# A decoder trunk with its residual stream turned round: tokens instead of features on partitions, and norms applied before the products

## The chip, the cores and the metric

One core of a Trainium2 chip runs the whole program. The metric is device time in microseconds of one execution, the median over runs of the same program. The core has a matrix engine (TensorE, PE in the profile; PEld is its loading of stationary operands), VectorE (DVE), ScalarE (ACT), GpSimd (POOL) and SyncE (SP), whose queue issues most transfers.

## The reference

512 tokens of 1024 features run through two layers in float32. Each layer is a half-step SwiGLU FFN (width 2816), a mixer, and another half-step FFN; every sub-layer has an RMS norm before it and one behind it, and is added to the residual stream. The mixer of layer 0 is a gMLP (chunked causal gating over 128 tokens, 16 groups); the mixer of layer 1 is multi-head latent attention (8 heads) whose keys and values come from the stream after layer 0.

```python
def rms_norm(x, g):
    y = x32 * lax.rsqrt(jnp.mean(x32 * x32, axis=-1, keepdims=True) + RMS_EPS) * g
...
for layer in range(DEPTH):
    f = swiglu(rms_norm(h, ffn_pre_g[layer, 0]), w_gate, w_up, w_down)
    h = h + 0.5 * rms_norm(f, ffn_post_g[layer, 0])
    n = rms_norm(h, mix_pre_g[layer])
    m = gmlp_mixer(n, ...) if layer < N_A_LAYERS else mla_mixer(n, k_nope, k_rope, v, ...)
    h = h + rms_norm(m, mix_post_g[layer])
    f = swiglu(rms_norm(h, ffn_pre_g[layer, 1]), w_gate, w_up, w_down)
    h = h + 0.5 * rms_norm(f, ffn_post_g[layer, 1])
    if layer == N_A_LAYERS - 1:
        k_nope, k_rope, v = shared_kv(h, ...)
```

## The kernel before

**Layout.** Everything lives with features on partitions: the residual stream `hall` is 8 chunks of 128 features by 512 tokens. A weight chunk of 128 x 128 is TensorE's stationary operand and 512 (or 256) tokens move.

**Precision.** Each float32 operand is split exactly into a high and a low float32r part; `mm3` makes a product of three TensorE instructions (high by high, high by low, low by high). A *unit* of weights is a transfer of some 512 KB into a raw buffer (`wr`, WR = 3 of them), then one ScalarE cast (`wh`) and one VectorE subtraction (`wl`) into split buffers (WS = 6 pairs). Activations share a pool of 59 slots of 128 x 512 (`a` in the profile).

**Order.** The program is a list of `Item`s, run in order by `Flow.drive`. Each names the units that it loads. `Flow` keeps an estimate of when each engine finishes each instruction. Ahead of each product, `Flow.reach` advances whatever waiting generator is due by that estimate, and `Flow.feed` splits units up to AHEAD = 4 items ahead where a split buffer is free and VectorE and ScalarE have little to do. `flow.hold` stops such splitting while a root is awaited. On the chip each engine then runs its instructions in the order that comes out, waiting on semaphores.

**Pre-norms are late.** `gained` splits h times the gain, not normed; the products of the next sub-layer start on that. The norm's scalar per token (`Norm`: R along tokens on all partitions, r by token, e) is made meanwhile: `Squares` sums squares of chunks (ScalarE, then adds on GpSimd), `token_mean` sums over features with TensorE (`mean` in the profile), `rsqrt` runs five small steps on GpSimd (`y`, `nt`, `r`), and `spread` lays the scalars along tokens with TensorE (`ident,r`). `glu`, `v_out`, `u_out` and the latent multiply by R or r behind the products. SwiGLU's up branch is not multiplied: the output then is f r, and the post-norm takes e = eps / r^2 in place of its epsilon.

**Seams.** `Boundary` is what lies between two sub-layers; there are b0 (input) to b6 (output), and five seams b1 to b5 have work on both sides. `project` computes a sub-layer's output, in groups of hidden features (FGROUPS) for an FFN. In the last group, HELD chunks of output (4, or 3 behind a mixer) keep their weights and run in two halves of 256 tokens, A and then B. `Boundary.finish` is started behind each half: token_mean, root, spread (`half,y`; `ident,y`), then for each chunk the post-norm, the residual sum, `gained` and the square for the next norm. While it runs for A, TensorE does the held chunks of B; while it runs for B, TensorE does the first three pairs of columns of the next FFN on A (`p` and `q` in `ffn`; `q` is loaded early into activation slots), or the first columns of the next mixer. At the end, `store` writes the last half by chunks of features.

**Shared keys.** `Shared.run` splits the stream after layer 0 again with `kv_norm`'s gain and multiplies by R behind the product.

Of the kernel before, what the change touches and what calls it, by code (L numbers as in the profile page):

```python
# [33 lines left out]
FGROUPS = ((0, 8), (8, 15), (15, 22))  # L34
# [23 lines left out]
for _name, _w in (  # L58
    ("ffn_pre", 32), ("ffn_post", 32), ("mix_pre", 16), ("mix_post", 16), ("kv_norm", 8),
    ("kv_a", 2), ("q_norm", 4), ("ln_g", 16), ("ln_b", 16), ("inv_freq", 1),  # L60
):
    COLS[_name] = _n
    _n += _w
# [13 lines left out]
def cost(engine, name, aps):  # L77
    """About how long an instruction takes, in microseconds."""
    n = max(int(np.prod(x.shape[1:])) for x in aps)
    if engine == "PE":  # L80
        n = int(np.prod(aps[0].shape[1:]))
        return max(n * (1 if aps[1].dtype in (F32R, BF16) else 4) / 2370.0, 0.03)
# [28 lines left out]
class Flow:  # L111
    """The order of the program. Work that waits for other engines is a generator, which yields what it
    waits for: a condition (a callable), tensors (a list) or an engine that has less than so much to
    do (a pair). What engines do is followed by an estimate of each instruction's time."""
# [28 lines left out]
    def place(self, key, t, us):  # L143
        """Takes the first time from t on in which the engine has nothing to do."""
# [14 lines left out]
    def idle(self, key, lead):  # L159
        """When the engine has less than lead to do."""  # L160
# [34 lines left out]
    def reach(self, t):  # L195
        """TensorE's next instruction can start at t: do what is due before."""
# [13 lines left out]
    def drive(self, items, fetch, parts):  # L210
        """Run the items. Units are fetched, and split into parts, before their time where there is room."""
# [48 lines left out]
class Parts:  # L260
    """The two parts of each chunk of a tensor, and which halves of the tokens have been written."""
# [13 lines left out]
def decoder_kernel(ctx: ExitStack, tc: tile.TileContext, a: dict, out: bass.AP):  # L275
# [14 lines left out]
    # names given, units split  # L290
# [29 lines left out]
    # tables and clocks of the engines that the first products wait for  # L320
# [19 lines left out]
    half = const.tile([P, P], F32, name="half")  # L340
    GP.tensor_scalar(half, ident, 0.5, None, op0=ALU.mult)
# [10 lines left out]
    hall = const.tile([P, NK, S], F32, name="h")  # L352
    h = [hall[:, c, :] for c in range(NK)]

    def load_x(lo, hi_, chunks=range(0, NK, 2)):
        xT = a["xT"].rearrange("(c p) t -> p c t", p=P)
        for c in chunks:
            nc.sync.dma_start(hall[:, c : c + 2, lo:hi_], xT[:, c : c + 2, lo:hi_])
            flow.dma += 0.75
            flow.write(hall[:, c : c + 2, lo:hi_], flow.dma + 2.0)  # L360

# [7 lines left out]
    def parts(raw, src, shape, spare=False):  # L369
        """The parts of each of a unit's chunks; `spare` units take room of activations."""  # L370
# [20 lines left out]
    def mm3(ps, w, x, start, stop):  # L391
        """ps += w^T x from the parts of w (stationary) and x (moving)."""
# [30 lines left out]
    def rsqrt(x, n, out=None):  # L423
        """1 / sqrt of a few columns."""
# [14 lines left out]
    def token_mean(acc, lo, hi_, n):  # L439
        """Means of acc's columns over n features, by token on partitions."""  # L440
# [5 lines left out]
    def spread(c, n, diag):  # L446
        """Per-token scalars (token on partition, one column a tile) along the free axis, on all partitions."""
# [8 lines left out]
    class Squares:  # L456
        """Sums of chunks' squares."""
# [14 lines left out]
    class Norm:  # L472
        """Scalars of a pre-norm: R along tokens on all partitions, r by token, e = eps / r^2."""

        def __init__(self):
            self.R = slot()
            self.r = small(NT, "r", 3)
            self.e = small(NT, "e", 3)
            self.squares = Squares()
            self.have, self.wide = set(), set()  # L480

        def finish(self, lo, hi_):
            n = (hi_ - lo) // P
            j0 = lo // P
# [6 lines left out]
            y = rsqrt(x, n, self.r[:, j0 : j0 + n])  # L491
            V.tensor_scalar(self.e[:, j0 : j0 + n], x, RMS_EPS, None, op0=ALU.mult)
            self.have.add(lo)
# [8 lines left out]
        def known(self, lo, hi_, wide=True):  # L502
            s = self.wide if wide else self.have
            return lambda: all(t in s for t in range(lo, hi_, 256))

    def gained(c, gains, outs, lo, hi_):
        """Split h[c] times each gain."""
        src = h[c][:, lo:hi_]
        for (name, base), parts in zip(gains, outs):
            g = col(name, base + c)  # L510
            hi, lw = parts.pairs[c]
            SC.activation(hi[:, lo:hi_], src, AF.Copy, scale=g)
            V.scalar_tensor_tensor(
                lw[:, lo:hi_], src, g, hi[:, lo:hi_].bitcast(F32), op0=ALU.mult, op1=ALU.subtract
            )
            parts.mark(c, lo, hi_)

    class Boundary:
        """Post-norm of a sub-layer's output, the residual sum, and what the next sub-layers read."""

        def __init__(self, post, factor, gains, held=0, last=False):
            self.post, self.factor, self.gains = post, factor, gains
            self.held, self.last = held, last
            self.f = self.outs = self.norm = None
            self.spot = None

        def evac(self, d, rng, ps, first, last):
            if self.f is None:
                self.f = [slot() for _ in range(NK)]
                self.squares = Squares(V if self.last else GP)  # L530
            lo, hi_ = rng
            f = self.f[d]
            with urgent() if self.last else nullcontext():
                if first:
# [694 lines left out]
    def next_unit(*x):  # L1229
        loaded[0] += 1  # L1230
        if loaded[0] == 4:
            load_x(*B)
# [79 lines left out]
```

## Time and profile before

| | |
|---|---|
| median of 3 runs | 2021.57 us (2020.59 to 2021.59) |
| profiled execution, first to last instruction | 2020.5 us |
| TensorE matmuls busy | 1976.6 us, 98%, 10064 instructions |
| VectorE busy | 951.7 us, 47% |
| ScalarE busy | 717.7 us, 36% |
| GpSimd busy | 218.3 us, 11% |
| moved by DMA | 184.94 MB, mean 92 GB/s |
| mean granted TensorE clock | 0.993 |

The profiled execution's own time is its span of 2020.5 us and the little that lies around it: the fastest run took 2020.59. Nearly every instruction is issued through one helper, so all carry line L100, and groups are told apart by the names of what they write and read: `mm<-a,wh` is a product into a bank with tokens moving and weights stationary, `mm<-wh,a` one with weights moving. TensorE's instructions overlap (the length of one holds its filling and draining), so the rate is read from the distance between starts.

### The profile page before, as it was taken

What the parts mean: (1) busy time and instruction counts of PE and PEld (TensorE: products, weight loads), DVE (VectorE), ACT (ScalarE), POOL (GpSimd) and SP (SyncE); (2) the same over time, 40 slices, a digit from 0 to 9 for tenths busy, and PEclk for the clock granted to TensorE, in tenths of its full rate; (3) what the DMA queues carried; (4) which work ended last, traced back from release to release, by engine and by line L of the source; (5) the groups of instructions that cost most, each with busy time, mean ns of one, the idle gap of its engine ahead of it and who ended that gap; (6) DMA issues with size and microseconds to landing.
All of it is one profiled execution on the core that took longest, in us unless ns stands there. A gap on an engine that the chain in (4) does not pass through costs nothing.

```text
span 2020.5 us, 25023 instructions
## 1 busy us (share of the span) xinstructions
PE 1976.6 (98%) x10064; PEld 1685.8 (83%) x10064; DVE 951.7 (47%) x1437; ACT 717.7 (36%) x1176; POOL 218.3 (11%) x358
## 2 busy tenths in 40 slices
PE   8999999999999999999999999999999999999997
PEld 8888888888888888888888888888878898888886
DVE  6443344635635642333465443343767554234434
ACT  5232223433333432222243332223566553222222
POOL 4000000510001400000041010000521150000001
PEclk9999999999999999999999999999999999999999
DMA  6233333142333133333322233333121213332321
GB/s 205 84 99 94 99 96 113 53 136 73 96 103 108 40 115 94 93 96 104 104 74 84 76 114 97 99 93 97 43 73 63 81 46 105 94 100 88 105 84 43
DMA packets 56149, 184.94 MB, mean 92 GB/s; under 512 B 6176, under 2 KB 10400, under 8 KB 56032
## 3 DMA queue, kind: packets, MB, share of 16 engines
q1 hardware_dynamic: 54016, 179.85, 29.0%
q0 software_dynamic: 720, 2.36, 0.4%
q8 instruction: 79, 1.29, 0.3%
q10 hardware_dynamic: 1296, 1.12, 0.2%
q14 instruction: 38, 0.31, 0.0%
HBM read 181.21 MB, written 2.10 MB: 91 GB/s over the span
## 4 chain that ended last, share of the span: by engine, by line
PE 89%; DVE 5%; POOL 3%; ACT 2%; issue 1%; DMA 0%; SPq 0%; DVEq 0%; POOLq 0%; ACTq 0%
PE mm L100 89%; DVE a L100 3%; ACT a L100 1%; DVE h L100 1%; POOL nt L100 1%; POOL y L100 1%; DVE wl L100 1%; POOL a L100 1%; ACT wh L100 0%; POOL a L931 0%; DMA h<-in_xT 0%; DMA wr<-in_mla_w_o 0%; DVE m L100 0%; DVE x L100 0%; POOL r L100 0%
## 5 line engine op out<-in xcount | busy, mean ns | idle before, releaser
L100 PE MATMUL mm<-a,wh 128*128 128x512 f32 (+1 forms) x5584 | 1568.7, 367 | 3.4 <-ACT wh L100 1.3
L100 PEld LDWEIGHTS mm<-a,wh 128*128 128x128 f32 x5584 | 1009.8, 189 | 171.6 <-DVE a L100 1.8
L100 PE MATMUL mm<-a,wl 128*128 128x512 f32 (+1 forms) x2792 | 1020.7, 366 | 1.5 <-DVE wl L100 1.5
L100 ACT CAST wh<-wr 128x1024 fp32r<-128x1024 f32 (+2 forms) x340 | 344.5, 1017 | 999.3 <-PE mm L100 713.2
L100 PEld LDWEIGHTS mm<-a,wl 128*128 128x128 f32 x2792 | 528.5, 189 | 86.0 <-DVE wl L100 2.0
L100 DVE TENSOR_TENSOR a<-mm,a 128x512 f32<-128x512 f32 (+3 forms) x380 | 228.6, 609 | 709.7 <-PE mm L100 698.9
L100 DVE TENSOR_TENSOR wl<-wr,wh 128x1024 fp32r<-128x1024 f32 (+2 forms) x340 | 403.4, 1190 | 216.4 <-ACT wh L100 204.2
L100 POOL TENSOR_TENSOR a<-a,a 128x256 f32<-128x256 f32 x162 | 139.6, 869 | 1165.7 <-ACT a L100 1162.3
L100 PE MATMUL mm<-a,a 128*128 128x256 f32 (+3 forms) x896 | 131.6, 299 | 2.3 <-ACT a L100 2.3
L100 ACT ACTIVATE a<-a 128x256 f32<-128x256 f32 (+1 forms) x216 | 105.5, 504 | 69.4 <-DVE a L100 68.9
L100 PEld LDWEIGHTS mm<-a,a 128*128 128x128 f32 x896 | 119.8, 191 | 7.5 <-ACT a L100 3.2
L100 DVE TENSOR_TENSOR a<-a,a 128x512 fp32r<-128x512 f32 (+4 forms) x171 | 107.9, 633 | 28.1 <-ACT a L100 21.2
L100 ACT CAST a<-a 128x512 fp32r<-128x512 f32 (+2 forms) x134 | 77.8, 583 | 75.6 <-DVE a L100 74.7
L100 PE MATMUL mm<-wh,a 128*128 128x512 f32 x288 | 93.0, 398 | 0.0
L100 POOL TENSOR_TENSOR y<-x,minus_half 128x2 f32<-128x2 f32 (+1 forms) x28 | 22.1, 788 | 527.7 <-DVE x L100 527.6
L100 ACT ACTIVATE a<-h,vec 128x256 fp32r<-128x256 f32 (+1 forms) x104 | 52.1, 520 | 52.6 <-DVE h L100 50.1
L100 PEld LDWEIGHTS mm<-wh,a 128*128 128x128 f32 x288 | 55.1, 191 | 11.7 <-issue 0.2
L100 DVE SCALAR_TENSOR_TENSOR a<-h,vec,a 128x256 fp32r<-128x256 f32 (+1 forms) x104 | 58.1, 578 | 6.0 <-ACT a L100 5.9
L100 PE MATMUL mm<-wl,a 128*128 128x512 f32 x144 | 56.8, 395 | 0.0
L100 DVE SCALAR_TENSOR_TENSOR h<-a,vec,h 128x256 f32<-128x256 f32 x80 | 48.2, 623 | 0.0
L100 ACT COPY a<-mm 128x512 f32<-128x512 f32 (+1 forms) x66 | 33.3, 512 | 32.7 <-PE mm L100 32.7
L100 DVE TENSOR_TENSOR a<-a,mm 128x256 f32<-128x256 f32 x94 | 36.2, 412 | 15.7 <-PE mm L100 13.4
(83 smaller groups left out, 453.0 us busy)
## 6 DMA issues: line engine op xcount, KB each, us to landing
wr<-in_ffn_w_up SPq DMA_DIRECT2D x88, 512.0 KB, 3.5
wr<-in_ffn_w_gate SPq DMA_DIRECT2D x87, 512.0 KB, 3.6
wr<-in_ffn_w_down SPq DMA_DIRECT2D x64, 448.0 KB, 3.3
wr<-in_ffn_w_down SPq DMA_DIRECT2D x32, 512.0 KB, 3.5
wr<-in_w_in_u SPq DMA_DIRECT2D x16, 512.0 KB, 3.7
wr<-in_w_in_v SPq DMA_DIRECT2D x16, 512.0 KB, 3.6
wr<-in_gmlp_w_out SPq DMA_DIRECT2D x16, 512.0 KB, 3.5
wr<-in_mla_w_o SPq DMA_DIRECT2D x8, 512.0 KB, 3.5
```

Source lines behind the costliest of these rows:

```text
L100: res = fn(*args, **kwargs)
```

## The change

The residual stream, the output projections and the norms have tokens on partitions; `hall` is 4 tiles of 128 tokens by 1024 features. In an output projection 128 tokens are the stationary operand and 512 output features of a weight unit (two chunks of 128 rows) move. Squares are summed along the free axis by ScalarE's accumulator, so no TensorE means or spreads are needed at the seams, and roots have one column. The next sub-layer's input is normed in full (`enter`), then turned back to features on partitions by TensorE transposes, from whose banks `gained` splits it (`turned`). So the scaling by R and r behind the products goes, except in the first FFN, whose input comes as before, and where the up branch now is scaled too. In the last group, HELD units (6, or 5 behind a mixer) keep their weights and run tile by tile over the four tiles; `finish` is started behind each tile. FGROUPS are of even widths. The post-norm gains are read as a row broadcast to all partitions; x is read by tokens as well, ahead of the twelfth unit. Slots go from 59 to 51 beside four tiles of 128 x 1024 (`f`). Flow's cost of TensorE instructions is changed a little. The file's comments and docstrings are gone too.

```diff
-FGROUPS = ((0, 8), (8, 15), (15, 22))
+FGROUPS = ((0, 8), (8, 16), (16, 22))
-WR, WS, SLOTS = 3, 6, 59
+WR, WS, SLOTS = 3, 6, 51
-HELD = (4, 3, 4, 4, 3, 4)
+HELD = (6, 5, 6, 6, 5, 6)
...
+        if name == "transpose":
+            return 0.125
+        return max((n + 31) * (1 if aps[1].dtype in (F32R, BF16) else 4) / 2400.0, 0.03)
...
     class Boundary:
+        def begin(self):
+            if self.post is not None:
+                self.gains = const.tile([P, D], F32, tag="post", name=nm("post"), bufs=1)
+                nc.gpsimd.dma_start(self.gains, a["post"][self.post].partition_broadcast(P))
+        def evac(self, t, e, ps, first, last):
+            if t not in self.f:
+                self.f[t] = wide(), small(2, "fs", NT)
+            f, ss = self.f[t]
+            r = slice(e * S, (e + 1) * S)
+            f = f[:, r]
+            if first and last:
+                SC.activation(slot(), ps, AF.Square, accum_out=ss[:, e : e + 1])
+                V.tensor_tensor(f, ps, self.gains[:, r], op=ALU.mult)
+                return
+            if first:
+                SC.copy(f, ps)
+            else:
+                V.tensor_tensor(f, ps, f, op=ALU.add)
+            if last:
+                SC.activation(slot(), f, AF.Square, accum_out=ss[:, e : e + 1])
+                if e == 0:
+                    V.tensor_tensor(f, f, self.gains[:, r], op=ALU.mult)
+                else:
+                    self.late.add(t)
+        def root(self, ss, factor):
+            x = small(1, "x")
+            k = 1.0 / factor**2
+            with urgent():
+                if ss.shape[1] > 1:
+                    GP.tensor_tensor(x, ss[:, :1], ss[:, 1:2], op=ALU.add)
+                    ss = x
+                GP.tensor_scalar(x, ss[:, :1], k / D, k * RMS_EPS, op0=ALU.mult, op1=ALU.add)
+            return rsqrt(x, 1)
+        def finish(self, t):
             self.open()
+            f, ss = self.f[t]
+            yield [ss]
+            y = self.root(ss, self.factor)
+            if t in self.late:
+                V.tensor_tensor(f[:, S:], f[:, S:], self.gains[:, S:], op=ALU.mult)
             yield [y]
+            if self.last:
+                for e in range(2):
+                    r = slice(e * S, (e + 1) * S)
+                    V.scalar_tensor_tensor(h[t][:, r], f[:, r], y, h[t][:, r], op0=ALU.mult, op1=ALU.add)
+                    (nc.sync, nc.scalar)[e].dma_start(out[t * P : (t + 1) * P, r], h[t][:, r])
+                return
+            V.scalar_tensor_tensor(h[t], f, y, h[t], op0=ALU.mult, op1=ALU.add)
+            yield from self.enter(t, f)
+        def enter(self, t, n):
+            ss = small(1, "hs", NT)
+            SC.activation(n, h[t], AF.Square, accum_out=ss)
+            yield [ss]
+            r = self.root(ss, 1.0)
+            yield [r]
+            SC.activation(n, h[t], AF.Copy, scale=r)
+            self.n[t] = n
+            t0 = t // 2 * 2
+            if t0 in self.n and t0 + 1 in self.n:
+                yield from self.turned((t0, t0 + 1), self.gain, self.outs[0])
+        def turned(self, ts, gain, parts):
+            lo, hi_ = ts[0] * P, (ts[-1] + 1) * P
+            w = hi_ - lo
+            each = S // w
+            for c0 in range(0, NK, each):
+                yield [self.n[t] for t in ts]
+                ps = bank()
+                for j in range(each):
+                    for i, t in enumerate(ts):
+                        PE.transpose(
+                            ps[:, j * w + i * P : j * w + (i + 1) * P],
+                            self.n[t][:, (c0 + j) * P : (c0 + j + 1) * P], ident,
+                        )
+                for j in range(each):
+                    gained(ps[:, j * w : (j + 1) * w], gain, parts, c0 + j, lo, hi_)
+                yield ("V", T_LEAD)
...
+    def project(source, ks, bnd, first, last, width=NK):
+        def some(unit, e, u, t):
...
+                mm3(banks[t, e], tokens(x, k, t * P, (t + 1) * P), unit[j], k == 0, k == width - 1)
+            if u == nu - 1:
+                bnd.evac(t, e, banks.pop((t, e)), first, last)
+        for e, u in units[: len(units) - held]:
+            item(lambda us, e=e, u=u: whole(us, e, u), load(e, u))
+        def block(us, e, u, t):
+            if us:
+                kept[e, u] = us[0]
+            some(kept[e, u], e, u, t)
+            if (e, u) == units[-1]:
+                flow.later(bnd.finish(t))
+        for t in range(NT):
+            for e, u in units[len(units) - held :]:
+                item(
+                    lambda us, e=e, u=u, t=t: block(us, e, u, t), load(e, u) if t == 0 else (),
+                    int(t == NT - 1),
+                )
...
         def glu(f, rng, pg, pu):
-            yield norm.known(lo, hi_)
-            V.tensor_tensor(g, pg, norm.R[:, lo:hi_], op=ALU.mult)
-            SC.activation(g, g, AF.Silu)
+            if norm is None:
+                yield [pg]
+                SC.activation(g, pg, AF.Silu)
+            else:
+                yield norm.known(lo, hi_)
+                R, u = norm.R[:, lo:hi_], slot()[:, : hi_ - lo]
+                V.tensor_tensor(g, pg, R, op=ALU.mult)
+                SC.activation(g, g, AF.Silu)
+                V.tensor_tensor(u, pu, R, op=ALU.mult)
+                pu = u
...
         if loaded[0] == 4:
-            load_x(*B)
+            load_xT(*B)
+        elif loaded[0] == 12:
+            for t in range(NT):
+                load_x(t)
```

More of the change, by code (lines that the diff above doesn't have):

```diff
@@ L349, in decoder_kernel, with load_x, wide @@
     GP.tensor_copy(identb, ident)
[L352 to L360, printed above, removed]
+    hall = const.tile([P, NT, D], F32, name="h")
+    h = [hall[:, t, :] for t in range(NT)]
+    def load_x(t):
+        nc.sync.dma_start(h[t], a["x"][t * P : (t + 1) * P, :])
+        flow.dma += 1.5
+        flow.write(h[t], flow.dma + 2.0)
+    def wide():
+        return act.tile([P, D], F32, tag="f", name=nm("f"), bufs=NT)
     def fetch(src, shape, spare=False):
@@ L500, in finish, with known @@
             self.wide.add(lo)
[L502 to L516, printed above, removed]
+        def known(self, lo, hi_):
+            return lambda: all(t in self.wide for t in range(lo, hi_, 256))
@@ L523, in __init__ @@
             self.held, self.last = held, last
[L524 removed]
+            self.f, self.outs, self.n, self.late = {}, None, {}, set()
+            self.norm = None
             self.spot = None
[L527 to L534, printed above, removed]
[L535 to L544 removed]
+        def begin(self):
+            if self.post is not None:
+                self.gains = const.tile([P, D], F32, tag="post", name=nm("post"), bufs=1)
+                nc.gpsimd.dma_start(self.gains, a["post"][self.post].partition_broadcast(P))
+                flow.write(self.gains, flow.now + 8.0)
@@ L549, in open @@
[L549 to L566 removed]
+                self.outs = [new_parts()]
@@ L1029, in latent_out @@
             x = small(n, "x")
-            V.tensor_tensor(x, ps[:, :n], norm.e[:, j0 : j0 + n], op=ALU.add)
+            V.tensor_scalar(x, ps[:, :n], RMS_EPS, None, op0=ALU.add)
             y = rsqrt(x, n)
```

227 lines of the change are left out of this document (91 added, 136 removed).

## The prediction

> **What bounds the kernel now.** I read the page's busy times first, then its chain that ended last.
>
> ```profile
> span 2020.5 us, 25023 instructions
> ...
> PE 1976.6 (98%) x10064; PEld 1685.8 (83%) x10064; DVE 951.7 (47%) x1437; ACT 717.7 (36%) x1176; POOL 218.3 (11%) x358
> ...
> PE 89%; DVE 5%; POOL 3%; ACT 2%; issue 1%; DMA 0%; SPq 0%; DVEq 0%; POOLq 0%; ACTq 0%
> ```
>
> TensorE bounds it: 98% of the span, 89% of the chain. An instruction saved on VectorE (47%) or ScalarE (36%) is worth nothing by itself. What counts is how many TensorE instructions there are, how long each holds it, and where it stands still. It stands still for 2020.5 - 1976.6 = 44 us. Next come windows around the five seams between sub-layers (columns: length, busy time by engine, granted clock, DMA).
>
> ```profile
> 364.00:404.00 40.00, 35.17 (x227) 31.94 (x227) 28.88 (x62) 21.10 (x46) 20.58 (x34) 0.91 0.13 40
> 660.00:710.00 50.00, 46.20 (x371) 44.49 (x370) 33.89 (x74) 24.38 (x53) 22.89 (x38) 1.00 0.11 33
> 1030.00:1080.00 50.00, 46.50 (x358) 45.28 (x357) 33.47 (x72) 21.36 (x49) 23.90 (x40) 0.93 0.14 43
> 1425.00:1510.00 85.00, 78.87 (x501) 69.61 (x500) 63.98 (x128) 49.77 (x111) 34.70 (x61) 0.98 0.21 63
> 1626.00:1656.00 30.00, 26.11 (x211) 25.09 (x210) 21.40 (x51) 17.62 (x41) 18.82 (x30) 1.00 0.12 36
> ```
>
> Length less the first busy figure is TensorE's idle time: 4.8, 3.8, 3.5, 6.1 and 3.9, together 22.2 us, half of all that it has. The waits say who ends most of it: the tail of the reciprocal root on GpSimd.
>
> ```profile
> PE mm L100 <- POOL y L100: 13.9, 12, 3.9
> ```
>
> A long wait also costs clock, as TensorE's timeline behind the 3.9 us one shows (start, length, count of merged instructions):
>
> ```profile
> 388.01 1.23 PE L100 MATMUL mm<-half,y 128*128 128x128 f32 x4 [3.95 <-POOL y L100]
> 388.89 0.77 PE L100 MATMUL mm<-wh,a 128*128 128x512 f32 x1
> ...
> 393.21 0.39 PE L100 MATMUL mm<-wl,a 128*128 128x512 f32 x1
> ```
>
> Ten products start between 388.89 and 393.21, 0.43 us each, where 0.227 is usual (below): 2.0 us lost. With clock 0.93 and 0.98 at two other seams I put the loss at 5 us in all (an estimate: 2, 2, 1).
>
> **The change, part by part.** The rates come from starts in TensorE's timeline, since its instructions overlap and their lengths don't add up.
>
> ```profile
> 367.07 0.28 PE L100 MATMUL mm<-a,wl 128*128 128x256 f32 x1
> ...
> 368.87 0.28 PE L100 MATMUL mm<-a,wl 128*128 128x256 f32 x1
> 368.99 0.50 PE L100 MATMUL mm<-mean,a 128*128 128x1 f32 x4
> 369.35 0.48 PE L100 MATMUL mm<-a,wh 128*128 128x256 f32 x2
> 369.67 0.28 PE L100 MATMUL mm<-a,wl 128*128 128x256 f32 x1
> ...
> 372.36 0.71 PE L100 MATMUL mm<-half,y 128*128 128x128 f32 x4 [0.26 <-POOL y L100]
> 372.83 0.36 PE L100 MATMUL mm<-a,wh 128*128 128x256 f32 x1
> ...
> 379.10 0.62 PE L100 MATMUL mm<-wh,a 128*128 128x512 f32 x2
> ...
> 381.14 0.62 PE L100 MATMUL mm<-wh,a 128*128 128x512 f32 x2
> ```
>
> Products of 256 columns: fifteen in 1.80 us, 0.120 each. Products of 512 columns with weights moving and tokens stationary, which is what every output projection becomes: nine in 2.04 us, 0.2267 each.
>
> *Projections.* Work is the same but for the held chunks, which ran in two 256-wide halves: 4 chunks x 7 x 3 x 2 = 168 in each of four FFNs and 3 x 8 x 3 x 2 = 144 in each mixer, 960 in all. They become 480 of 512: 480 x (0.240 - 0.2267) = **-6.4 us**. The Trainium skill ("TensorE: Matmul & The Clock Gate", section "Wait — 56ns, not 53.3ns?") gives a warm product N / 2.4 GHz and about 2.5 ns; by that a pair of halves costs 2.5 ns more than the whole, not 13, and this term would be -1.2 us. The trace's fixed part is about 13 ns, so I keep the rows.
>
> *Norm scalars.* Means over features (mean) and the spreading of scalars (half,y; ident,y; ident,r) leave six post-norms and five pre-norms, two halves each: 22 times. One mean holds TensorE from 368.99 to 369.35, 0.36 us, and the two products behind it take 0.32 where 0.24 is usual; a spread holds it for 0.47, and I charge the same 0.08 behind it. 22 x (0.36 + 0.08 + 0.47 + 0.08) = **-21.8 us**.
>
> *Transposes.* 8 chunks x 4 tiles at each of five seams and for the shared keys: 192 of 128 x 128. The nearest are attention's:
>
> ```profile
> 1528.97 1.15 PE L100 MATMUL mm<-ident,a 128*128 128x128 f32 x9
> 1529.87 0.36 PE L100 MATMUL mm<-a,a 128*128 128x256 f32 x1
> ...
> 1538.45 1.45 PE L100 MATMUL mm<-ident,a 128*128 128x128 f32 x9
> 1539.65 0.60 PE L100 MATMUL mm<-a,a 128*128 128x256 f32 x3
> ```
>
> Nine in 0.90 or in 1.20 us: 0.100 to 0.133, middle 0.117, so 22.4 us; in 48 groups of four, each with 0.08 for the switch, 3.8 more. **+26.2 us**, bounds 19 and 30.
>
> *Waits at the seams.* Before, each half stops TensorE's queue at up to four places. After, none of the next sub-layer's products can start on unnormed tokens, and one place is left in each half: the first transposes, which stand in TensorE's in-order queue until the two tiles' whole chain is done, with all products written behind them waiting. The chain by rows:
>
> ```profile
> 369.77 0.72 POOL y L100
> 370.56 0.92 POOL nt L100
> ```
>
> ```profile
> L100 DVE TENSOR_TENSOR a<-mm,a 128x512 f32<-128x512 f32 x234 | 161.6, 691 | 635.0 <-PE mm L100 634.3 <-ACT a L100 0.7
> L100 DVE TENSOR_TENSOR wl<-wr,wh 128x1024 fp32r<-128x1024 f32 x264 | 325.4, 1234 | 210.7 <-ACT wh L100 201.6
> L100 DVE SCALAR_TENSOR_TENSOR a<-mm,vec,a 128x256 fp32r<-128x256 f32 x8 | 3.6, 474 | 0.0
> L100 ACT CAST wh<-wr 128x1024 fp32r<-128x1024 f32 x264 | 277.2, 1052 | 752.3 <-PE mm L100 474.2 <-issue 260.9 <-DMA wr<-in_gmlp_w_out 6.5
> L100 ACT ACTIVATE a<-a 128x512 f32<-128x512 f32 x92 | 57.8, 629 | 7.8 <-DVE a L100 7.8
> L100 ACT ACTIVATION_READ_ACCUMULATOR a<-mm,m 128x1 f32 x32 | 6.3, 196 | 0.0
> ```
>
> A root of five GpSimd steps ran from 369.77 to the spread at 372.36, 2.6 us; with one and with two steps more (0.25 each, an estimate from that) 2.85 and 3.1. Chain: add 0.69, square 0.63 + 0.20, root 3.1, residual sum over 1024 (as wl) 1.23, square over 1024 (as wh) 1.05 + 0.20, root 2.85, scaling 1.05: 11.0. Then four transposes 0.45 and the two split steps at 0.47: **12.4 us** to the first chunk. Cover: the first half has two tiles' blocks of six units, 2 x 6 x 2 x 3 x 0.2267 = 16.3 us (13.6 with five units, behind the mixers); the second half has three pairs of columns of the first, 144 x 0.120 = 17.3 us. On average the chain is hidden, with 1 to 5 us to spare; on ScalarE and VectorE weight splits of 1.05 and 1.23 us now stand between its steps, because the change drops flow.hold, which kept them back during a root. VectorE's residual sum waits for GpSimd; behind it in order stand other tiles' sums and weight subtractions, and those feed TensorE. No row shows a chain of that length, so I bound it: 0 (hidden) to 3.9 us (longest wait above) a half. I take 1.16, the mean of the root's waits (13.9 / 12), the nearest row: 10 x 1.16 = 11.6 us, and 1 us of clock.
>
> *Weights behind the seams.* Held units fill all six split buffers; before, two stayed free. A next FFN needs four units at its first chunk, only three fit into the raw buffers, and the fourth transfer waits until the first is split.
>
> ```profile
> wr<-in_ffn_w_up SPq DMA_DIRECT2D x88, 512.0 KB, 3.5
> ```
>
> The last tile takes 8.16 us. The order cuts the first unit two blocks into it, at 2.7; 1.05 + 1.23 makes 5.0, the transfer 8.5, the next 1.05 and 1.23 make 9.6 and 10.8. TensorE reaches the fourth unit's products at 8.16 + 9 x 0.12 = 9.2, its low part at 9.5: 1.4 us late, bounds 0 and 5. Three such seams: **+4.5 us**. The other two take the fourth unit later.
>
> Seams together: 11.6 + 1 + 4.5 - 22.2 - 5 = **-10.1 us**.
>
> *The end.*
>
> ```profile
> 2005.87 0.28 PE L100 MATMUL mm<-a,wl 128*128 128x256 f32 x1
> ...
> 2015.98 0.75 DVE L100 TENSOR_TENSOR h<-h,a 128x256 f32<-128x256 f32 x2
> ```
>
> Last product at 2006.15, last sum at 2016.73, span end at 2020.5: 10.6 us of chain and 3.8 us of storing. After: add 0.69, square 0.83, root 3.1 (as above, GpSimd being quieter here perhaps less), two sums of 0.75, hand-overs about 0.3, storing 3.8: 10.2 for 14.4, **-4.2 us**, bounds -6 and -2 (the store moves 256 KB a piece, not 128).
>
> *At nothing.* The R multiplications that leave gelu, silu and the latent, the one more in the first FFN (0.69 us x 25), the gain multiplications and squares: VectorE and ScalarE are half idle, and if that cover went, each would cost its 0.4 to 0.7 us. GpSimd loses the sums of squares and gets about 13 tiny steps a tile. x is read again by tokens, four transfers of 512 KB on SP's queue ahead of the twelfth unit, about 6 us later for that unit, which isn't cut until five more columns' products (over 20 us) have run. Six loads of gains on GpSimd's queue lie a whole projection ahead of use. Fewer activation slots could couple attention's steps; no row prices that, 0 to 5 us, I take 0.
>
> Sum: -6.4 - 21.8 + 26.2 - 10.1 - 4.2 = -16.3. Against the span, 2020.5 - 16.3 = 2004.2; the median of the runs lies 1.1 above it, and so I forecast 2005 us.
>
> **The rivals.** With s as the wait per half, the time is 2021.6 - 6.4 - 21.8 + 26.2 - 4.2 + (1 + 4.5 - 22.2 - 5) + 10 s = 1993.7 + 10 s. A measurement tells 0.2%, 4 us, from no change: faster means s under 2.4, slower means s over 3.2.
> (1) *Everything hidden*: the computed margins suffice, s is under 0.4 and the weights come in time. At s = 0: 1993.7 - 4.5 = 1989, and 1982 with the transposes at their bound of 19. For it: the computed covers, and one stopping place where there were four. Against: in this order waits arose although work was queued.
> (2) *The seams eat it up*: s from 2.4 to 3.2, 2017.7 to 2025.7: the waits only change their place. For it: 2.2 us a half stand there now (22.2 / 10), and the new chain is longer than any now. Against: four stopping places a half become one.
> (3) *Slower: the full chain isn't covered.* One mechanism: the chain runs late behind weight splits in ScalarE's and VectorE's queues (two splits on each are 4.6 us more), TensorE stands at the transposes. It decides from s = 3.2 on; at s = 4 it is 2034, and since a 3.95 us stop halved the clock for 4 us, 10 x 2 us more could come: up to 2054. For it: margins of 1.2 us behind the mixers. Against: no wait in the trace is longer than 3.9.
> (4) *GpSimd's roots locked out.* Its small steps vary:
>
> ```profile
> L100 POOL TENSOR_TENSOR nt<-nt,x x28: 196/199/1455, 22.0 to 2009.6; 128x2 f32<-128x2 f32 x26, 128x4 f32<-128x4 f32 x2
> ```
>
> The median is 0.2 us, the longest 1.455, as long as one VectorE subtraction more. If two steps of every root hit that, the chain is 2 x 2 x 1.25 = 5 us longer, and since the written order doesn't reckon with it, nearly all of that falls on TensorE: s about 4.5, 2039. The Trainium skill ("SBUF — State Buffer", section "Who interferes with whom") says that a VectorE instruction with two SBUF inputs and a GpSimd one that reads SBUF block each other for a whole instruction; the spread of that row agrees, its median says that it is rare.
>
> **How the numbers follow.** Forecast (s 0.4 to 2.4): 0.54, its own range 1997 to 2017. Rival 1: 0.20. Rival 2: 0.10. Rival 3: 0.12. Rival 4: 0.04. Faster is forecast and rival 1, 0.74; same 0.10; slower 0.16. Range for 8 in 10: from 1988, which cuts a quarter of rival 1 (0.05), to 2026, which cuts rivals 3 and 4 but for their start (0.15).
>
> **What would show it.** Held projections: no 256-wide rows left but in the gate, up, u, latent and score products. Norm scalars: mean, ident,r rows left only for the first norm, the shared latent and the queries; half,y gone. Transposes: 272 rows mm<-ident,a (80 + 192), starting 0.10 to 0.13 apart. Seams: in the windows around the five seams TensorE's idle time falls from 22.2 to about 17 us, its waits now ended by ScalarE (the scaling), not by GpSimd; a wait for wh or wl at three of them. End: 10 us from last product to span end. Wrong it would be if those waits pass 3 us each, if transposes start over 0.2 apart, or if attention's stretch grows.

## The result: 0.8% slower

The changed kernel takes 2037.41 us (median of 4 runs, 2036.63 to 2037.70) where the kernel before takes 2021.14 (4 runs): a ratio of 1.008, 95% interval 1.0066 to 1.0095. 2005 with 1988 to 2026 was forecast, so both the sign and the range were missed.

### The profile page after: what moved, and what is told of

It is laid out like the page before. It is cut to its first block, busy times and chain, and to the rows that moved or that the text cites. A ratio compares the mean times of both kernels' runs of the same rounds, so it can differ in the third digit from the quotient of the medians.

```text
span 2034.9 us, 23641 instructions
## 1 busy us (share of the span) xinstructions
PE 1977.5 (97%) x9600; PEld 1665.6 (82%) x9600; DVE 867.2 (43%) x1179; ACT 710.0 (35%) x1117; POOL 154.7 (8%) x397
## 4 chain that ended last, share of the span: by engine, by line
PE 85%; POOL 5%; ACT 3%; issue 3%; DVE 3%; DMA 1%; SPq 0%; POOLq 0%; DVEq 0%; ACTq 0%
PE mm L102 85%; POOL y L102 2%; ACT a L102 2%; POOL nt L102 2%; ACT f L102 1%; DVE h L102 1%; POOL x L102 1%; DVE a L102 1%; DVE wl L102 1%; POOL a L102 0%; DMA wr<-in_ffn_w_up 0%; ACT wh L102 0%; DVE f L102 0%; POOL a L962 0%; DMA wr<-in_mla_w_o 0%
## 5 line engine op out<-in xcount | busy, mean ns | idle before, releaser
L102 PE MATMUL mm<-a,wh 128*128 128x512 f32 (+1 forms) x3472 | 1006.1, 374 | 23.5 <-ACT a L102 13.3
L102 PEld LDWEIGHTS mm<-a,wh 128*128 128x128 f32 x3472 | 637.3, 191 | 137.8 <-ACT a L102 15.9
L102 ACT CAST wh<-wr 128x1024 fp32r<-128x1024 f32 (+1 forms) x332 | 343.2, 1036 | 922.7 <-PE mm L102 650.9
L102 PE MATMUL mm<-wh,a 128*128 128x512 f32 x2080 | 649.8, 391 | 9.8 <-ACT a L102 7.2
L102 DVE TENSOR_TENSOR wl<-wr,wh 128x1024 fp32r<-128x1024 f32 (+1 forms) x332 | 400.7, 1209 | 580.7 <-ACT wh L102 565.1
L102 PE MATMUL mm<-a,wl 128*128 128x512 f32 (+1 forms) x1736 | 645.5, 372 | 1.3 <-DVE wl L102 1.2
L102 PEld LDWEIGHTS mm<-wh,a 128*128 128x128 f32 x2080 | 391.3, 188 | 92.0 <-ACT a L102 7.8
L102 PE MATMUL mm<-wl,a 128*128 128x512 f32 x1040 | 405.6, 390 | 0.0
L102 PEld LDWEIGHTS mm<-a,wl 128*128 128x128 f32 x1736 | 330.9, 191 | 57.3 <-DVE wl L102 2.2
L102 PEld LDWEIGHTS mm<-wl,a 128*128 128x128 f32 x1040 | 195.9, 188 | 40.3 <-issue 0.2
L102 DVE TENSOR_TENSOR a<-a,a 128x512 fp32r<-128x512 f32 (+4 forms) x182 | 117.4, 646 | 28.3 <-ACT a L102 19.2
```

The lines of the kernel that those rows point to most:

```text
L102: res = fn(*args, **kwargs)
```

## The profile after

The changed kernel's page, busy times and chain:

```profile
span 2034.9 us, 23641 instructions
...
PE 1977.5 (97%) x9600; PEld 1665.6 (82%) x9600; DVE 867.2 (43%) x1179; ACT 710.0 (35%) x1117; POOL 154.7 (8%) x397
...
PE 85%; POOL 5%; ACT 3%; issue 3%; DVE 3%; DMA 1%; SPq 0%; POOLq 0%; DVEq 0%; ACTq 0%
```

464 TensorE instructions fewer, and yet TensorE's share of the chain falls from 89% to 85%, while GpSimd's and ScalarE's shares rise: work went, waits came. The five windows around the seams, in the columns used before:

```profile
364.00:412.00 48.00, 40.79 (x206) 34.23 (x206) 24.68 (x36) 25.73 (x47) 21.31 (x52) 0.93 0.38 121
662.00:712.00 50.00, 43.26 (x290) 40.09 (x288) 23.78 (x38) 24.78 (x48) 14.65 (x40) 0.93 0.19 64
1030.00:1080.00 50.00, 43.59 (x274) 39.73 (x273) 27.04 (x42) 26.17 (x52) 16.39 (x46) 0.93 0.22 74
1430.00:1515.00 85.00, 74.49 (x437) 64.69 (x436) 46.42 (x80) 46.98 (x94) 24.47 (x58) 0.98 0.20 63
1640.00:1672.00 32.00, 26.01 (x143) 21.88 (x142) 16.23 (x21) 17.61 (x33) 13.22 (x40) 0.95 0.31 99
```

TensorE's idle time there is 7.2, 6.7, 6.4, 10.5 and 6.0, together 36.9 us (22.2 before). The time lost below full clock, each length times one less the granted clock (the sixth figure behind the length), is 3.4 + 3.5 + 3.5 + 1.7 + 1.6 = 13.7 us (by the same reading 8.8 before). The waits, TensorE's own:

```profile
PE mm L102 <- ACT a L102: 22.8, 12, 6.3
PE mm L102 <- DVE a L102: 14.5, 14, 2.6
PE mm L102 <- POOL y L102: 3.5, 5, 1.5
PE mm L102 <- POOL a L102: 3.2, 3, 1.7
PE mm L102 <- DVE wl L102: 1.2, 3, 0.5
...
PE mm L102 <- ACT f L102: 0.7, 2, 0.5
```

This list holds the answer. `f` is a normed tile, what the transposes read; `a` is, at the seams, a chunk split behind the transposes, what the next products read (`ACT a` its high part, `DVE a` its low part; 6.0 us of these two rows lie outside the five windows). TensorE hardly ever waited *at* the transposes (0.7 us); it waited at the first products behind them, for the splits. How that came about shows at seam b1, in TensorE's timeline and then ScalarE's (start, length, instruction, the idle time before it and what ended it):

```profile
374.49 0.60 PE L102 MATMUL mm<-ident,f 128*128 128x128 f32 x4
374.84 0.48 PE L102 MATMUL mm<-wh,a 128*128 128x512 f32 x1
375.15 0.40 PE L102 MATMUL mm<-wl,a 128*128 128x512 f32 x1
...
378.83 0.39 PE L102 MATMUL mm<-wh,a 128*128 128x512 f32 x1
385.49 0.80 PE L102 MATMUL mm<-wh,a 128*128 128x512 f32 x1 [6.27 <-ACT a L102]
386.08 0.63 PE L102 MATMUL mm<-wl,a 128*128 128x512 f32 x1
...
389.50 0.63 PE L102 MATMUL mm<-wl,a 128*128 128x512 f32 x1
```

```profile
374.23 1.98 ACT L102 CAST wh<-wr 128x1024 fp32r<-128x1024 f32 x2
378.44 1.06 ACT L102 ACTIVATE f<-h 128x1024 f32<-128x1024 f32 x1 [2.23 <-DVE h L102]
379.41 0.18 ACT L102 ACTIVATION_READ_ACCUMULATOR f<-h 128x1 f32 x1
379.50 1.03 ACT L102 CAST wh<-wr 128x1024 fp32r<-128x1024 f32 x1
383.31 1.15 ACT L102 ACTIVATE f<-h,y 128x1024 f32<-128x1024 f32 x1 [2.79 <-POOL y L102]
384.37 0.61 ACT L102 ACTIVATE a<-f 128x512 f32<-128x512 f32 x1
384.89 0.19 ACT L102 ACTIVATION_READ_ACCUMULATOR a<-f 128x1 f32 x1
384.98 0.45 ACT L102 ACTIVATE a<-mm,vec 128x256 fp32r<-128x256 f32 x1
```

The first half's first four transposes start at 374.49; the first of their splits (`a<-mm,vec`) starts at 384.98, 10.1 us after TensorE has gone on to its next product at 374.84. In between ScalarE runs the chain of *tile 2*: its square (`f<-h`, 2.23 us waiting for VectorE's sum), its scaling (`f<-h,y`, 2.79 waiting for GpSimd's root), and tile 3's half square; what is left of two weight casts, and a third one, take some 2.4 us of it. In program order these stand ahead of the splits. TensorE uses up the products that need no split and stands for 6.27 us, then runs products at half speed (nine starts from 386.08 to 389.50, 0.43 us apart, where 0.227 is usual; granted clock 0.50 from 385.5 to 390). The Trainium skill ("Perfetto Trace Analysis", section "Tensor Engine Instruction (MATMUL, LD_WEIGHTS)") says that ScalarE, VectorE and GpSimd run their queues strictly in order; these rows agree, since finished transposes lay there for 10 us and were not taken first. Seam b3 shows the same rows in the same order, with one wait of 6.23 us. At b2, b4 and b5 the longest waits are 2.3, 2.6 and 2.3 us; at b2 one split comes ahead of tile 2's square on ScalarE, and its low part on VectorE stands behind tile 2's residual sum and a weight subtraction.

## Experiments

Three theories were to be told apart. *Queues*: the splits of a half stand in ScalarE's and VectorE's in-order queues behind steps of later tiles' chains, which wait for roots. *Weights*: the products that should cover the chain wait for split weights that come late. *Length* (latency, in the expectations): the chain is simply too long for its cover. In each edit the lines marked - are the changed kernel's.

**1. const_scale.** The scaling stays where it is in ScalarE's order, but waits for no root.

```diff
-            SC.activation(n, h[t], AF.Copy, scale=r)
+            SC.activation(n, h[t], AF.Copy, scale=0.25)
```

> The next sub-layer's input is scaled by a constant instead of the pre-norm's root (the pre-norm is left out of the result; the root itself is still computed); order of instructions on ScalarE as in the changed kernel. Queue theory (the splits behind the transposes stand in ScalarE's in-order queue behind the scaling of a later tile, which waits for GpSimd's root): the scaling of tile 2 waits no longer, so the first split comes 3 to 4 us sooner at most seams; TensorE's idle time at the five seams falls from 37 to about 20 us, time about 2021 us (2016 to 2027). Weights theory (all six split buffers held, the next weights late): no change, 2037 us. Latency theory (the chain itself is too long for its cover): each half is 2.9 us sooner where it was late, 2012 to 2025 us.

Measured: 2015.24 us, 0.9973 of the kernel before (0.9964 to 0.9982), so 22 us less than the changed kernel. ScalarE at the same seam, b1 (the first row is tile 2's square, the second its scaling, now `f<-h` too):

```profile
378.44 1.06 ACT L102 ACTIVATE f<-h 128x1024 f32<-128x1024 f32 x1 [2.24 <-DVE h L102]
...
380.43 1.05 ACT L102 ACTIVATE f<-h 128x1024 f32<-128x1024 f32 x1
381.39 0.61 ACT L102 ACTIVATE a<-f 128x512 f32<-128x512 f32 x1
381.91 0.19 ACT L102 ACTIVATION_READ_ACCUMULATOR a<-f 128x1 f32 x1
382.00 0.45 ACT L102 ACTIVATE a<-mm,vec 128x256 fp32r<-128x256 f32 x1
```

The transposes start at 374.89 here, 0.4 us later than in the changed kernel, and the split 3 us earlier, as the theory of the queues expected. Tile 2's square still stands ahead of it and waits 2.24 us for VectorE. TensorE's idle time in windows around the five seams is 22.9 us, where about 20 was expected. The time lies just under the range of the queues (2016 to 2027) and inside that of length (2012 to 2025), so this run doesn't tell the two apart; it rules out the weights (2037). The wait for the pre-norm's root is one part of the cost, not all.

**2. no_root_waits.** As 1, and the residual sum waits for no root either.

```diff
-            V.scalar_tensor_tensor(h[t], f, y, h[t], op0=ALU.mult, op1=ALU.add)
+            V.scalar_tensor_tensor(h[t], f, 0.001, h[t], op0=ALU.mult, op1=ALU.add)
...
-            SC.activation(n, h[t], AF.Copy, scale=r)
+            SC.activation(n, h[t], AF.Copy, scale=0.25)
```

> As const_scale, and the residual sum takes a constant too (post-norm and pre-norm are left out of the result at the seams; the roots are still computed, nobody waits for them). Queue and latency theory: no engine waits for a root at a seam any more; seam idle time under 10 us, time 2005 to 2014 us. Weights theory: 2037 us.

Measured: 1991.95 us, 0.9856 (0.984 to 0.9873). That is 13 us below the range of queues and length (2005 to 2014), so both had put the cost of root waits too low. All work is there (each engine has as many instructions as in the changed kernel), only the waits for roots are gone, and with them nearly all idle time at the seams (windows at the same five places):

```profile
355.00:405.00 50.00, 50.00 (x261) 42.81 (x260) 30.14 (x43) 29.55 (x54) 28.94 (x64) 1.00 0.36 108
645.00:695.00 50.00, 50.00 (x346) 46.51 (x345) 27.51 (x44) 27.54 (x52) 23.07 (x53) 1.00 0.20 64
1010.00:1060.00 50.00, 50.00 (x349) 46.71 (x348) 27.01 (x42) 24.90 (x50) 19.27 (x45) 1.00 0.24 74
1395.00:1480.00 85.00, 79.48 (x467) 68.98 (x466) 50.01 (x84) 48.81 (x99) 32.85 (x70) 1.00 0.21 63
1600.00:1640.00 40.00, 39.81 (x272) 36.63 (x271) 21.64 (x35) 24.74 (x48) 15.58 (x45) 1.00 0.25 79
```

5.7 us idle instead of 36.9, nearly all of it in the fourth window, and a granted clock of 1.00 throughout. The 31.2 us of idle time and the 13.7 of lowered clock that are gone make up 44.9 of the 45.5 us between the two kernels. So the weights cost next to nothing: 45 us hang on waits for roots. Which of two ways they take, the chain's length or the queues, this run doesn't tell.

**3. pair_roots.** Tiles 2 and 3 share their roots (two columns) in one `finish`, started behind tile 3; nothing is left out. Tile 2's steps come later in the queues, and the second half's chain gets no shorter. (`finish_pair` and the sums that the two tiles share are not shown.)

```diff
-                flow.later(bnd.finish(t))
+                if bnd.last or t < 2:
+                    flow.later(bnd.finish(t))
+                elif t == 3:
+                    flow.later(bnd.finish_pair())
```

> Tiles 2 and 3 share their roots, so that the squares and scalings of tile 2 wait for the end of tile 3 and come behind the first half's splits in ScalarE's queue; the chain of the first half is as long as in the changed kernel, that of the second half about 3.5 us longer. Queue theory: the 6 us waits of the first halves go, seam idle time 37 to about 20 us, time about 2021 us (2015 to 2027). Latency theory: nothing gained in the first half, the second half later, 2037 to 2047 us. Weights theory: 2037 us.

Measured: 2017.63 us, 0.9984 (0.9975 to 0.9994): 19.8 us less than the changed kernel, inside the range of the queues. Seam b1, ScalarE:

```profile
375.23 2.93 ACT L102 CAST wh<-wr 128x1024 fp32r<-128x1024 f32 x3
379.29 0.63 ACT L102 ACTIVATE a<-f 128x512 f32<-128x512 f32 x1 [1.12 <-DVE f L102]
379.83 0.19 ACT L102 ACTIVATION_READ_ACCUMULATOR a<-f 128x1 f32 x1
379.92 0.45 ACT L102 ACTIVATE a<-mm,vec 128x256 fp32r<-128x256 f32 x1
```

TensorE there:

```profile
375.49 0.60 PE L102 MATMUL mm<-ident,f 128*128 128x128 f32 x4
...
380.43 0.50 PE L102 MATMUL mm<-wh,a 128*128 128x512 f32 x1 [0.23 <-ACT a L102]
...
1655.09 0.48 PE L102 MATMUL mm<-ident,f 128*128 128x128 f32 x1 [3.81 <-ACT f L102]
```

The transposes start at 375.49, later than in the changed kernel, and the split at 379.92, five us earlier: only weight casts and tile 3's half square stand between. TensorE's first product behind it waits 0.23 us, not 6.27, and the wait of 6.23 at b3 is gone too. In windows around the five seams TensorE's idle time is 21.6 us, where about 20 was expected, and the time lost below full clock 4.9 us, where it was 13.7. The last row is the longest wait left, for the second half behind a mixer. Sharing roots also takes 65 of 397 instructions off GpSimd, so order is not all that changed; but at b1 the first half's transposes came no sooner for it. This is what the theory of the queues says, and a longer chain with a faster kernel is what the theory of length can't give.

**4. held_fewer.** Less cover for the chain, and four instead of six split buffers held, so that weights come earlier.

```diff
-HELD = (6, 5, 6, 6, 5, 6)
+HELD = (4, 3, 4, 4, 3, 4)
```

> HELD back to 4 and 3 units, two split buffers stay free at a seam, a tile's blocks take 5.4 us instead of 8.2. Weights theory: the next weights come in time, 2025 to 2030 us. Queue theory: the splits still stand behind tile 2's scaling, and there is less cover: the waits grow, 2040 to 2060 us. Latency theory: cover of the first half 10.9 us against a chain of 12.4 us, 2045 to 2070 us.

Measured: 2062.43 us, 1.0205 (1.019 to 1.022). The waits:

```profile
PE mm L102 <- ACT a L102: 29.7, 11, 11.5
PE mm L102 <- ACT f L102: 19.2, 7, 6.3
```

The time is inside the range of length (2045 to 2070) and 2.4 us above that of the queues (2040 to 2060). Two blocks less of cover a tile cost 25 us, and freed split buffers don't make up for that; since the edit changes both, it is run 2 and the short waits for `wl` that acquit the weights. Now TensorE does wait at the transposes (`ACT f`, 19.2 against 0.7): with six held units the chain up to there was covered, with four it isn't. So the chain's length counts as soon as its cover goes.

**5. pair_roots_held6.** Pairing, and a sixth held unit behind the mixers too, where pairing left the longest wait at the transposes (3.8 us).

```diff
-HELD = (6, 5, 6, 6, 5, 6)
+HELD = (6, 6, 6, 6, 6, 6)
```

> pair_roots with six held units behind the mixers too, so that the cover of the first half there is 16.3 us instead of 13.6. If what is left in pair_roots at these two seams (waits of 4.5 and 5.4 us) is a chain longer than its cover, 3 to 6 us go: about 2013 us (2011 to 2016). If it is order again, nothing: 2017 to 2019 us.

Measured: 2014.81 us, 0.9965 (0.9952 to 0.9977), 2.8 us below pairing alone and inside the range for a chain longer than its cover. At the two seams behind the mixers, TensorE's waits over 0.25 us ahead of the second half's transposes fall from 6.0 us to 1.2. At the second half's transposes, whose cover this edit leaves as it is, it waits 4.1 us at b2 (nothing with pairing alone) and 2.0 at b5 (3.8).

**6. scale_on_gpsimd.** The scaling leaves ScalarE's queue altogether; it stands on GpSimd behind the root that it needs.

```diff
-            SC.activation(n, h[t], AF.Copy, scale=r)
+            GP.tensor_scalar(n, h[t], r, None, op0=ALU.mult)
```

> In the changed kernel the pre-norm's scaling of 128x1024 moves from ScalarE to GpSimd, which makes the root itself; ScalarE then waits for no root, tiles keep roots of their own. Queue theory: ScalarE's splits come 2 to 3 us sooner, but its squares still wait for VectorE's residual sum, which waits for a root: 2022 to 2032 us. Latency theory: the scaling takes longer on GpSimd (1.3 to 3.6 us by its rows for 512 elements), so later, 2038 to 2060 us.

Measured: 2040.47 us, 1.0093 (1.0079 to 1.0107): the theory of the queues expected 2022 to 2032 and missed, and the time lies at the lower end of what length expected (2038 to 2060). GpSimd's timeline at b1 says why:

```profile
364.12 2.86 POOL L102 TENSOR_SCALAR f<-h,y 128x1024 f32<-128x1024 f32 x1
366.95 0.19 POOL L102 TENSOR_TENSOR x<-fs 128x1 f32<-128x1 f32 x1
```

The scaling takes 2.86 us there (1.15 on ScalarE), and GpSimd has a queue too: the next tile's root starts only when it ends, at 366.95, though ScalarE had its sum of squares ready at 364.65, and the sum on VectorE and the square on ScalarE then wait for that root. The blockage was moved, not taken away. That fits the mechanism, but the forecast had overlooked it; as a test between the theories this run is weak.

**7 to 9. Late norm.** If the waits for roots are the cost, the pre-norm's root and scaling can leave the chain: transposes turn h itself, and r multiplies behind the products, as in the kernel before. Its root is shared by two tiles, and TensorE spreads r again (four instructions a half). `squared` sums the squares of h, and `prenorm` makes a half's root and spreads it to `norm.R`.

```diff
-            ss = small(1, "hs", NT)
-            SC.activation(n, h[t], AF.Square, accum_out=ss)
-            yield [ss]
-            r = self.root(ss, 1.0)
-            yield [r]
-            SC.activation(n, h[t], AF.Copy, scale=r)
-            self.n[t] = n
...
+            self.squared(t, n)
+            if t == 1:
+                flow.later(self.prenorm(0))
...
+            self.n[t] = h[t]
...
+            bc = spread(y, 2, ident)
...
-            SC.activation(us_[g][:, lo:hi_], ps, AF.Gelu_apprx_tanh)
+            u = us_[g][:, lo:hi_]
+            V.tensor_tensor(u, ps, prev.norm.R[:, lo:hi_], op=ALU.mult)
+            SC.activation(u, u, AF.Gelu_apprx_tanh)
```

Run 7, late_norm_pair, has this on top of pairing (3):

> pair_roots, and the pre-norm applied behind the products as in the kernel before (R along tokens, r by token, spread by TensorE); the transposes turn the residual stream itself. The chain to the first split loses one root and the scaling (3.9 us), TensorE gets ten spreads of two tiles (about 5.5 us). Latency as the rest of the loss: seam waits fall from about 22 to 8 us, 2008 to 2014 us. If the rest is order: 2018 to 2026 us (the spreads are paid, nothing is gained).

Measured: 2005.26 us, 0.9916 (0.9902 to 0.9929), faster than both kernels, and 3 us below the better of the two ranges, that of length (2008 to 2014). TensorE and ScalarE at b1:

```profile
370.02 1.03 PE L102 MATMUL mm<-ident,h 128*128 128x128 f32 x8
```

```profile
370.65 0.47 ACT L102 ACTIVATE a<-mm,vec 128x256 fp32r<-128x256 f32 x1 [0.56 <-PE mm L102]
```

The transposes come 4.5 us earlier than in the changed kernel, and the split follows 0.6 us behind their start, waiting for nothing but them. The edit shortens the chain and takes the scaling out of ScalarE's queue at once; it doesn't say how much each is worth.

Run 8, late_norm, is the late norm with each tile's `finish` as in the changed kernel:

> The changed kernel with the pre-norm applied behind the products, roots of the post-norm by single tiles (one part of the change undone, without pair_roots). No scaling stands in ScalarE's queue any more, and six of the first half's eight splits come ahead of tile 2's square in it. Queue theory: pairing was needed only for the scaling's sake, so the time is that of late_norm_pair, 2003 to 2009 us. If late_norm_pair owed its gain to the pairing, 2015 to 2025 us.

Measured: 2011.94 us, 0.9951 (0.9938 to 0.9965), between its two ranges, 3 us above what the theory of the queues expected (2003 to 2009). Even without the scaling, the later tiles' squares and sums stand in the queues and wait for the post-norm's root; that fits the 6.7 us that pairing is still worth.

Run 9, late_pair_held6, is run 7 with the edit of run 5:

> late_norm_pair with six held units behind the mixers too. The chain is now some 9 us against covers of 13.6 us, so more cover should gain nothing: 2003 to 2007 us. If waits at these seams still come from cover, 2000 to 2002 us.

Measured: 2006.31 us, 0.9926 (0.9913 to 0.9938): no gain over run 7, as expected. With the chain shorter, five units cover it behind a mixer.

Together: from the changed kernel's 2037.4, pairing takes 19.8 us (3), the pre-norm's root and scaling off the chain 12.4 more (7), and 13 are left to the kernel that waits for no root (2). The runs were timed in three sets, in which the kernel before took 2021.12, 2021.93 and 2021.46 us. So both theories hold a part: the queues are shown by run 3, which the theory of length can't give, and that length counts too by runs 4 and 5; the weights are ruled out. How the last 25 us divide between queues and length stays open.

## Why the prediction was wrong, step by step

*Projections*, forecast -6.4: right. The 960 instructions of 256 columns are gone and 480 of 512 came. At full clock and without waits the median distance between starts is 0.120 us for 256 columns and 0.227 for 512 in both traces, so 480 x 0.227 - 960 x 0.120 = -6.2. By the rule of the Trainium skill that the prediction weighed there it would have been -1.2; the rows decide, and they held.

*Norm scalars*, forecast -21.8: right. From each start to the next, means fell from 14.2 to 2.6 us and spreads from 12.7 to 1.8, -22.5 (2.6 us of the means before are waits behind them).

*Transposes*, forecast +26.2: nearly right, 1.7 too much. The changed kernel's group:

```profile
L102 PE MATMUL mm<-ident,f 128*128 128x128 f32 x192 | 30.1, 289 | 0.7 <-ACT f L102 0.7
```

192 take 21.2 us by starts, 0.110 each, where 22.4 was forecast. The charge for the switch behind a group was right, 0.085 us on average at full clock: at b1 the product at 374.84 holds TensorE for 0.31 us instead of 0.227. But there are 39 groups instead of 48, which makes 3.3 us, and 24.5 in all.

*The end*, forecast -4.2: right in sign, 1.4 short. The last product and the last sums:

```profile
2025.67 0.39 PE L102 MATMUL mm<-wh,a 128*128 128x512 f32 x1
```

```profile
2030.35 1.41 DVE L102 SCALAR_TENSOR_TENSOR h<-f,y,h 128x512 f32<-128x512 f32 x2 [2.08 <-POOL y L102]
```

From the product's end, 2026.06, to the span's end, 2034.9, it is 8.8 us (14.4 before), -5.6.

*Weights behind the seams*, forecast +4.5: wrong, and it didn't matter. Waits for `wl` come to 1.2 us in the whole kernel, 0.5 the longest; the kernel before has 1.5.

*Waits at the seams*: **this step failed.** The chain's length came out, in part by luck: at b1 tile 1's last product ends at 362.40 and its scaling at 373.71, 11.3 us for a forecast of 11.0, but its two roots were shorter than reckoned (2.69 and 2.12 us against 3.1 and 2.85), and 1.2 us went in ScalarE's queue, where its half square stood behind tile 0's scaling. The transposes start at 374.49, between products that TensorE still had, so the cover hid the chain (0.7 us of waits at the transposes in the whole kernel). The error is in the sentence that takes that end for the end of the wait ("then four transposes 0.45 and the two split steps at 0.47: 12.4 us to the first chunk"). The split steps were put directly behind the transposes; in ScalarE's queue they come behind the next tiles' chains, 10 us later at b1. The prediction saw such queueing ahead of the transposes ("behind it in order stand other tiles' sums"), priced it with the mean wait of a root, 1.16 us, and looked for the stop at the transposes alone. Put into its own sum, 1993.7 + 10 s = 2037.4, s is 4.4 us, above the 3.9 that it held for the longest. That bound ("no wait in the trace is longer than 3.9") was read from the old order, and the new order had waits of 6.27 and 6.23 us.

By direct reading the seams cost 14.7 us more idle time and 4.9 us more of lowered clock, where together -10.1 was forecast: a miss of nearly 30 (some idle time lies at lowered clock, so the two overlap a little). Norm scalars, transposes and the end gave back 3.8. Two things that the prediction put at nothing add to it: the first FFN, where a mean waits 1.7 us for GpSimd and the same product (the last of the first 96 `mm<-a,a`) starts at 52.0 us instead of 48.9, and attention, whose stretch from its first `mm<-a,a` to its last is 1.0 us longer (102.9 against 101.9). That adds up to the miss of 30.7 us between the spans within about a microsecond.

*The rivals.* The third, slower by queues on ScalarE and VectorE, came nearest in mechanism, with 2034 at s = 4. It was half right: in-order queues, but what stands in them and waits is the later tiles' chains, not weight splits, and TensorE stood at the products, not at the transposes. The first, everything hidden, forecast 1989 without waits for roots and weights; run 2 gave 1992, so the sum without its seam term was right within 3 us, though with misses on both sides (transposes and the end below, the first FFN and attention above). The fourth, GpSimd locked out, has the nearest number, 2039, but by luck. At b1 two steps of tile 2's pre-norm root took 1.05 and 1.03 us instead of 0.19. Here is the second and the VectorE subtraction beside it:

```profile
381.43 1.03 POOL L102 TENSOR_TENSOR nt<-y 128x1 f32<-128x1 f32 x1
```

```profile
381.19 1.22 DVE L102 TENSOR_TENSOR wl<-wr,wh 128x1024 fp32r<-128x1024 f32 x1
```

Both end within 0.05 us of each other, as the lock that the prediction cited from the Trainium skill would have it. That was 1.7 us at this seam; over the whole kernel the `nt<-y` steps of one column took 12.0 us for 44, 0.27 each. The first step of the post-norm's root shows it more often (shortest, median and longest in ns):

```profile
L102 POOL TENSOR_TENSOR x<-fs x24: 193/697/1127, 355.8 to 2027.6; 128x1 f32<-128x1 f32 x24
```

In 17 of its 24 instances it takes about 0.70 us and ends within 0.1 us of VectorE's `f<-f,post`, which starts just ahead of it. All steps of one column together take 25 us more than at their shortest, 0.57 a root for 44 roots, where the rival had reckoned with 2.5.

*Signs to look for.* Held projections and norm scalars appeared as told, transposes at 0.11 apart, the end at 9 us, and the waits at the seams are ended by ScalarE, though by its splits and not by the scaling. The waits for weights at three seams didn't come. Idle time at the seams was to fall to 17 us and rose to 36.9, 3.7 a half. Of the marks of a wrong prediction two came: single waits passed 3 us at two of the five seams, and attention's stretch grew, by 1.0 us.

## What to carry to other kernels

When an edit moves a step, follow what it *produces* to its consumer and read what stands ahead of that consumer in its own engine's queue; a chain's length doesn't contain that. An instruction that waits for a small root holds up all that is written behind it on its engine, so a later tile's waiting steps belong behind an earlier tile's ready ones: here that was worth 20 us. And where a longest wait in the old trace serves as a bound, ask whether the old order could have shown a longer one at all.

## What the runs showed of the hardware

A stop of 6.27 us was followed by products 0.43 us apart till the next transposes, nine starts' worth, which cost some 1.8 us on top of the stop; the granted clock from 385.5 to 390 was 0.50. A scaling of 128 x 1024 float32 by a scalar per token took 2.86 us on GpSimd and 1.15 on ScalarE. Every accumulating activation on ScalarE in this trace is followed by a read of the accumulator of 0.18 to 0.20 us. A GpSimd step of one column that takes 0.19 us alone took 0.70 beside VectorE's `f<-f,post` and 1.03 or more beside its weight subtraction, and ended with it. And a kernel with 464 TensorE instructions fewer, whose terms outside the seams were nearly all as forecast, ran 0.8% slower; with two tiles' roots paired it ran 0.2% faster than the kernel before.
